# HGRN scores with the keys of two sequence tiles in one stationary operand, the odd tile's reversed

## The chip, the cores and the metric

The kernel runs on one core of one Trainium2 chip. The metric is device time in microseconds (us) of one execution, lower is better. Engines are named as in the profile: PE is TensorE (matrix products), PEld its weight loads, DVE is VectorE, ACT is ScalarE, POOL is GpSimd and SP is SyncE, which here only issues transfers. A product has a stationary operand, which is loaded into the array first, and a moving operand, which is streamed through it; the result goes to one of eight banks of PSUM, each 128 partitions by 512 float32 values.

## What is computed

The reference is a two-layer decoder trunk on x of shape 1 x 512 x 2048 (float32). Layer 0 runs two recurrent branches beside each other, RG-LRU and HGRN2; layer 1 is differential attention. The change is in the HGRN2 branch, with 16 heads of 128 key features and 128 value features:

```python
def hgrn2_chunkwise(q, k, v, log_f):
    ...
    def step(state, inp):
        qc, kc, vc, gc = inp
        b = jnp.cumsum(gc, axis=2)
        o_inter = jnp.einsum('bhtk,bhkv->bhtv', qc * jnp.exp(b), state)
        decay = jnp.exp(jnp.where(mask, b[:, :, :, None, :] - b[:, :, None, :, :], -jnp.inf))
        scores = jnp.einsum('bhtk,bhsk,bhtsk->bhts', qc, kc, decay)
        o = o_inter + jnp.einsum('bhts,bhsv->bhtv', scores, vc)
        b_last = b[:, :, -1:, :]
        state = (jnp.exp(b_last[:, :, 0, :, None]) * state
                 + jnp.einsum('bhsk,bhsv->bhkv', kc * jnp.exp(b_last - b), vc))
        return state, o
```

The score of query t and key s is a sum over the 128 features of q(t) k(s) exp(b(t) - b(s)), for s not after t. The decay depends on the feature, so that a plain product of queries and keys does not give it.

## The kernel before

**Tiling.** The 512 positions are four tiles of 128. Features lie on the partitions, positions on the columns, so that a work tile of a head is 128 x 512.

**The scores by levels.** `hgrn_head` (line 196) splits exp(b(t) - b(s)) at a position between s and t. At level h (32, 16, 8, 4, 2) the positions fall into pairs of neighbouring blocks of h; the first block of a pair holds keys, the second queries, and b at the last key splits the exponent. `decays(h)` (233) makes one tile `e` of 128 x 512 for a level: keys times their part of the decay in the key columns (DVE line 239), queries times theirs in the query columns (238 and 241), with one exponential for both (ACT, 240). `score_mm` (244) then multiplies, for levels 16 to 2, the 128 columns of each tile by themselves: stationary and moving operand are the same 128 columns, four products a level (254). Of the 128 x 128 results only key rows against query columns of the same pair are wanted; `score_out` (256) copies these into the head's score tile `st` under a mask `msk` (268). Level 32 has eight products of 32 keys by 32 queries (249) and two copies (260), and the step of 64 has four of 64 by 64 (337) and a copy by ACT (342). Neighbours (h = 1) and the diagonal come from products of a matrix of ones in the fp32r format (279 to 282), where the diagonal is taken out by the identity (284).

**What follows.** `kp` holds the keys for the state that goes on to the next tile; it is transposed (339) into `so`. The state is built from `so` and v (350), and the output from `st`, v, `qp` and the states (365, 367). The output is normed and transposed (383), and handed on as `yb`. In all of these float32 products the trace has two matmul records for one product in the code, and one for one transpose; a record is called a pass below.

**Where the work stands.** The weights come in chunks of 512 KB on SP's queue (`raw`, 80), and each half chunk is split by ACT and DVE into two fp32r parts (`split`, 87; lines 91 and 92). `proj_feat` (126) and `proj_tok` (141) run 12 products of 512 columns for one half chunk (lines 104 to 106) and then call `tick`, which lets the generators in `mids` take `ticks` steps; a `yield` ends a step. `hgrn` (393) runs over eight pairs of heads: three feature projections a pair, and for each even pair a token projection that makes v for four heads. The two heads of a pair are worked out during the projections of the next pair, 2.1 steps for a half chunk in odd pairs and 1.3 in even ones (line 407). A head has 24 steps. Instructions are emitted in this order, but the framework's planner sorts each engine's list anew from its own estimate of when each is ready, with the order of the program as priority (splits first); at run time each engine then keeps its list.

**The start.** x, transposed, is loaded into the buffers yb0 to yb7, from which the normed input is scaled into `h` (804, 805). `prepare` (157) loads x again, untransposed, through POOL's queue into the same buffers as they come free (167), squares it on ACT (168), and works out the norm; it waits 10 steps first, and 5 more before its transposes (182). The tables `cst` (798) and `msk` (810) go through SP's queue between the loads of x and the later weight chunks.

Of the kernel before, what the change touches and what calls it, by code (L numbers as in the profile page):

```python
# [19 lines left out]
P = 128  # L20
# [27 lines left out]
K_ID, K_COS, K_SIN, K_NEG = 0, 128, 192, 256  # L48
N_CST = 384


class Kernel:
# [104 lines left out]
    def prepare(self):  # L157
# [4 lines left out]
        for _ in range(10):  # L162
            yield
        for i in range(8):
            xt = self.ybp.tile([P, 2 * S], F32, name=f"yb{(i + 2) % 8}")
            t, hf = i // 2, i % 2
            nc.gpsimd.dma_start(xt, self.x[t * P:(t + 1) * P, hf * 1024:(hf + 1) * 1024])
            nc.scalar.activation(xt, xt, AF.Square, accum_out=ss0[:, i:i + 1])
            yield
# [8 lines left out]
        for _ in range(5):  # L178
            yield
# [16 lines left out]
    def hgrn_head(self, hd, qs, f, sg, v, vc):  # L196
# [6 lines left out]
        k = wk.tile([P, S], F32, name="k")  # L203
# [26 lines left out]
        def vw(t, h):  # L230
            return t.rearrange("p (n two h) -> p n two h", two=2, h=h)

        def decays(h):
            n = S // (2 * h)
            e = wk.tile([P, S], F32, name="e", bufs=3)
            e0, e1 = vw(e, h)[:, :, 0, :], vw(e, h)[:, :, 1, :]
            mid = vw(b, h)[:, :, 0, h - 1:h].broadcast_to([P, n, h])
            V.tensor_tensor(e1, vw(b, h)[:, :, 1, :], mid, op=ALU.subtract)
            V.tensor_tensor(e0, vw(lnk, h)[:, :, 0, :], mid, op=ALU.add)  # L239
# [4 lines left out]
        def score_mm(h, e, ps):  # L244
            if h == 32:
                for t in range(NT):
                    for o in (0, 64):
                        c = t * P + o
                        nc.tensor.matmul(ps[o:o + 32, t * 32:(t + 1) * 32], e[:, c:c + 32], e[:, c + 32:c + 64],
                                         start=True, stop=True)  # L250
                return
            for t in range(NT):
                sl = slice(t * P, (t + 1) * P)
                nc.tensor.matmul(ps[:, sl], e[:, sl], e[:, sl], start=True, stop=True)  # L254

        def score_out(li, h, ps):
            if h == 32:
                ev, pv = st.rearrange("p (a c) -> p a c", a=NT), ps.rearrange("p (a c) -> p a c", a=NT)
                for o in (0, 64):
                    V.tensor_copy(ev[o:o + 32, :, o + 32:o + 64], pv[o:o + 32])  # L260
                return
            n4 = P // (2 * h)

            def v4(t):
                return t.rearrange("p (a n two h) -> p a n two h", a=NT, two=2, h=h)[:, :, :, 1, :]

            mk = self.msk[:, li * 64:(li + 1) * 64].rearrange("p (n h) -> p n h", h=h)
            V.copy_predicated(v4(st), mk.unsqueeze(1).broadcast_to([P, NT, n4, h]), v4(ps))

        def bank():  # L270
# [5 lines left out]
        yield  # L276
        st = wk.tile([P, S], F32, name="st")
# [5 lines left out]
        score_mm(32, e32, p2[:, 256:384])  # L283
        V.tensor_tensor(st.rearrange("p (a c) -> p a c", a=NT), ps.rearrange("p (a c) -> p a c", a=NT),
                        self.ident.unsqueeze(1).broadcast_to([P, NT, P]), op=ALU.mult)
        V.copy_predicated(st.rearrange("p (a n two) -> p a n two", a=NT, two=2)[:, :, :, 1],
                          self.msk[:, 64 * len(LEVELS):].unsqueeze(1).broadcast_to([P, NT, 64]),
                          p2[:, 0:256].rearrange("p (a n) -> p a n", a=NT))
        score_out(0, 32, p2[:, 256:384])
# [3 lines left out]
        e4 = decays(4)  # L293

# [3 lines left out]
        kq = wk.tile([P, S], F32, name="e128")  # L298
        ke = kq[:, 0:256].rearrange("p (c t) -> p c t", t=64)
        qo = kq[:, 256:512].rearrange("p (c t) -> p c t", t=64)  # L300

        def c64(t):
            return t.rearrange("p (c two t) -> p c two t", two=2, t=64)

        yield
        ps, p2 = bank(), bank()
        score_mm(16, e16, ps)
        score_mm(8, e8, p2)
        score_out(1, 16, ps)
        score_out(2, 8, p2)  # L310
        yield
        e2 = decays(2)
        yield
        be = b.rearrange("p (c t) -> p c t", t=64)[:, :, 63]
        dc = sm.tile([P, 12], F32, name="dc")
        V.tensor_copy(dc[:, 0:8], be)
        V.tensor_tensor(dc[:, 8:12], be[:, 0:8:2], be[:, 1:8:2], op=ALU.add)
# [666 lines left out]
```

## Time and profile before

| | |
|---|---|
| median of 3 runs | 2590.29 us (2589.52 to 2590.51) |
| profiled execution | 2592.2 us, of which the profiled span is 2590.4 us |
| granted TensorE clock | 0.999 of full speed |
| ACT busy | 1254.9 us of the span |
| DVE busy | 1413.8 us of the span |

The durations below come from the profiled execution. A matmul's duration in the trace runs from its start to its modelled end; products overlap, so that the distance between two starts, not the duration, is what a product costs in a row of them.

### The profile page before, as it was taken

The page shows a single profiled execution, that of the slowest core. Times are in us where ns is not written, and L with a number is a line of the kernel's source. Part 1 is how long each engine was busy: PE and PEld are TensorE (multiplying, and loading weights), DVE is VectorE, ACT ScalarE, POOL GpSimd, SP SyncE. Part 2 cuts the span into 40 slices and gives each one's busy share as a digit, 9 for nine tenths or more (in the row PEclk, how much of TensorE's full clock was granted, in tenths as well). Part 3 has the DMA queues.
Part 4 walks back from the last instruction along what each step waited for, and adds up shares of the span by engine and source line. Part 5 has one row for each costly group of instructions (what it writes and reads, how often), then busy time and mean ns, then how long its engine had stood idle before and what let it go on. Part 6 is the DMA issues. An engine that isn't in the chain of part 4 may idle for free.

```text
span 2590.4 us, 33188 instructions
## 1 busy us (share of the span) xinstructions
PE 2572.1 (99%) x12416; PEld 2134.4 (82%) x12416; DVE 1413.8 (55%) x3074; ACT 1254.9 (48%) x2456; POOL 4.6 (0%) x12
## 2 busy tenths in 40 slices
PE   9999999999999999999999999999999999999999
PEld 6888888888888888888888888888888888888887
DVE  5475656556657666555554555344534534544654
ACT  7354545445445465455544444344434434434543
POOL 0000000000000000000000000000000000000000
PEclk9999999999999999999999999999999999999999
DMA  6222222222222232232233333222222222222243
GB/s 243 98 82 74 82 83 79 83 78 78 82 84 72 74 106 98 98 98 98 90 122 98 131 122 128 97 91 81 79 93 82 75 96 82 79 93 92 87 147 114
DMA packets 73889, 250.48 MB, mean 97 GB/s; under 512 B 8192, under 2 KB 8960, under 8 KB 73728
## 3 DMA queue, kind: packets, MB, share of 16 engines
q1 hardware_dynamic: 72000, 243.56, 28.0%
q0 software_dynamic: 1152, 4.19, 0.4%
q8 instruction: 97, 1.59, 0.3%
q10 hardware_dynamic: 576, 0.61, 0.1%
q14 instruction: 64, 0.52, 0.1%
HBM read 239.95 MB, written 8.39 MB: 96 GB/s over the span
## 4 chain that ended last, share of the span: by engine, by line
PE 95%; ACT 2%; DVE 1%; issue 1%; DMA 1%; SPq 0%; POOL 0%; DVEq 0%; ACTq 0%; POOLq 0%
PE pj L104 28%; PE pj L106 28%; PE pj L105 28%; PE pm L254 2%; PE pm L614 1%; PE pm L104 1%; PE pm L106 1%; PE pm L105 1%; PE pm L365 1%; ACT a L726 0%; PE pm L594 0%; PE pm L367 0%; PE pm L350 0%; PE pm L337 0%; PE pm L638 0%
## 5 line engine op out<-in xcount | busy, mean ns | idle before, releaser
L92 DVE TENSOR_TENSOR wlo<-wraw,whi 128x512 fp32r<-128x512 f32 x848 | 583.0, 689 | 727.6 <-ACT whi L91 709.1
L91 ACT CAST whi<-wraw 128x512 fp32r<-128x512 f32 x848 | 523.5, 618 | 813.0 <-PE pj L106 482.6
L104 PE MATMUL pj<-whi 128*128 128x512 f32 x768 | 299.6, 391 | 0.0
L106 PE MATMUL pj<-whi,wlo 128*128 128x512 f32 x768 | 299.6, 390 | 0.0
L105 PE MATMUL pj<-wlo,whi 128*128 128x512 f32 x768 | 299.2, 390 | 0.0
L104 PEld LDWEIGHTS pj<-whi 128*128 128x128 f32 x768 | 144.3, 188 | 30.2 <-issue 0.5
L106 PEld LDWEIGHTS pj<-whi,wlo 128*128 128x128 f32 x768 | 144.2, 188 | 30.2 <-DVE wlo L92 0.2
L105 PEld LDWEIGHTS pj<-wlo,whi 128*128 128x128 f32 x768 | 144.3, 188 | 29.3
L92 DVE TENSOR_TENSOR wlo<-ya,whi 128x512 fp32r<-128x512 f32 x64 | 44.3, 693 | 91.2 <-ACT whi L91 91.2
L240 ACT ACTIVATE e<-e 128x512 f32<-128x512 f32 x80 | 50.6, 632 | 88.6 <-DVE e L239 88.4
L91 ACT CAST whi<-ya 128x512 fp32r<-128x512 f32 x64 | 39.7, 621 | 100.9 <-PE pj L105 100.9
L92 DVE TENSOR_TENSOR wlo<-y,whi 128x512 fp32r<-128x512 f32 x64 | 44.2, 691 | 77.4 <-ACT whi L91 77.4
L91 ACT CAST whi<-y 128x512 fp32r<-128x512 f32 x64 | 39.9, 623 | 92.5 <-PE pj L105 90.1
L92 DVE TENSOR_TENSOR wlo<-yb,whi 128x512 fp32r<-128x512 f32 x64 | 44.2, 691 | 69.7 <-ACT whi L91 69.4
L91 ACT CAST whi<-yb 128x512 fp32r<-128x512 f32 x64 | 39.8, 621 | 78.3 <-PE pj L105 78.2
L254 PEld LDWEIGHTS pm<-e 128*128 128x128 f32 x512 | 62.1, 191 | 2.4
L254 PE MATMUL pm<-e 128*128 128x128 f32 x512 | 62.3, 275 | 0.0
L619 ACT ACTIVATE p<-pm,mx 128x128 f32<-128x128 f32 (+3 forms) x64 | 33.5, 527 | 34.3 <-DVE mx L617 29.5
L726 ACT ACTIVATE a<-pj,rstd 128x128 f32<-128x128 f32 x128 | 47.5, 421 | 0.5
L241 DVE TENSOR_TENSOR e<-e,hin 128x256 f32<-128x256 f32 x80 | 34.0, 425 | 22.1 <-ACT e L240 20.9
L616 DVE TENSOR_REDUCE mx<-pm 128x1 f32<-128x128 f32 (+3 forms) x64 | 29.6, 484 | 11.3 <-PE pm L615 11.3
L562 DVE SCALAR_TENSOR_TENSOR a<-a,rs_y,row 128x128 f32<-128x128 f32 x128 | 35.6, 347 | 0.0
(473 smaller groups left out, 6448.4 us busy)
## 6 DMA issues: line engine op xcount, KB each, us to landing
wraw<-in_w_rec SPq DMA_DIRECT2D x191, 512.0 KB, 3.3
wraw<-in_w_att SPq DMA_DIRECT2D x128, 512.0 KB, 3.2
wraw<-in_w_rout SPq DMA_DIRECT2D x64, 512.0 KB, 3.3
wraw<-in_w_aout SPq DMA_DIRECT2D x32, 512.0 KB, 3.3
yb<-in_x POOLq DMA_DIRECT2D x8, 512.0 KB, 7.4
wraw<-in_w_gate SPq DMA_DIRECT2D x8, 512.0 KB, 3.2
xo<-in_x SPq DMA_DIRECT2D x16, 256.0 KB, 4.6
x1d<-xo SPq DMA_DIRECT2D x16, 256.0 KB, 4.0
```

What stands on the lines that cost most here:

```text
L91: self.nc.scalar.copy(hi, src)
L92: self.nc.vector.tensor_tensor(lo, src, hi.bitcast(F32), op=ALU.subtract)
L104: mm(out, a[0], b[0], start=start, stop=False)
L105: mm(out, a[0], b[1], start=False, stop=False)
L106: mm(out, a[1], b[0], start=False, stop=stop)
L240: nc.scalar.activation(e, e, AF.Exp)
L241: V.tensor_tensor(e1, e1, vw(qs, h)[:, :, 1, :], op=ALU.mult)
L254: nc.tensor.matmul(ps[:, sl], e[:, sl], e[:, sl], start=True, stop=True)
L562: V.scalar_tensor_tensor(sl, sl, rs[:, t * 4 + g:t * 4 + g + 1], gain, op0=ALU.mult, op1=ALU.mult)
L616: V.tensor_reduce(mx[:, i:i + 1], ps[:, :n], axis=AX.X, op=ALU.max)
L619: nc.scalar.activation(e[:, :n], ps[:, :n], AF.Exp, scale=ATT_SCALE, bias=mx[:, i:i + 1], accum_out=z[:, i:i + 1])
L726: nc.scalar.activation(x[:, t, g * P:(g + 1) * P], ps[t][:, g * P:(g + 1) * P], AF.Square, scale=r1, accum_out=ss[:, t * 4 + g:t * 4 + g + 1])
```

## The change

Keys sit in every other block of h columns. Read backwards, the keys of a tile fall into the other blocks. So 64 keys of an even tile at their own places and 64 keys of the following odd tile, backwards, fill one stationary operand of 128 columns; the moving operand is the 64 queries of the one and the 64 of the other. One product then serves two tiles, at every level from 64 to 2, and a mask that is mirrored for the odd tile takes the wanted entries. The rows of the odd tiles in `st` and in `kp` are thereby backwards, so v's odd tiles are turned round too, once for four heads, by a product with a reversal matrix that is added to `cst`.

```diff
-K_ID, K_COS, K_SIN, K_NEG = 0, 128, 192, 256
-N_CST = 384
+K_ID, K_REV, K_COS, K_SIN, K_NEG = 0, 128, 256, 320, 384
+N_CST = 512
...
-        for _ in range(10):
+        for _ in range(14):
             yield
         for i in range(8):
-            xt = self.ybp.tile([P, 2 * S], F32, name=f"yb{(i + 2) % 8}")
+            xt = self.ybp.tile([P, 2 * S], F32, name=f"yb{(i + 5) % 8}")
...
-        for _ in range(5):
+        for _ in range(7):
             yield
...
-        k = wk.tile([P, S], F32, name="k")
+        k = wk.tile([P, S], F32, name="st")
...
+        def packed(e):
...
+            ev = e.rearrange("p (u x) -> p u x", u=2)
+            return ev[:, :, 0:P], ev[:, :, P:2 * P]
 
         def decays(h):
-            n = S // (2 * h)
             e = wk.tile([P, S], F32, name="e", bufs=3)
-            e0, e1 = vw(e, h)[:, :, 0, :], vw(e, h)[:, :, 1, :]
-            mid = vw(b, h)[:, :, 0, h - 1:h].broadcast_to([P, n, h])
-            V.tensor_tensor(e1, vw(b, h)[:, :, 1, :], mid, op=ALU.subtract)
-            V.tensor_tensor(e0, vw(lnk, h)[:, :, 0, :], mid, op=ALU.add)
+            ks, qu = packed(e)
+            n, m = P // (2 * h), P // h
+            qu = qu.rearrange("p u (m h) -> p u m h", h=h)
+            mid = vw(b, h)[:, :, :, 0, h - 1:h]
+            V.tensor_tensor(qu, vw(b, h)[:, :, :, 1, :], mid.broadcast_to([P, 2, m, h]), op=ALU.subtract)
+            for par, kv in ((0, ks), (1, ks[:, :, ::-1])):
+                mine = slice(par * n, (par + 1) * n)
+                V.tensor_tensor(kv.rearrange("p u (n two h) -> p u n two h", two=2, h=h)[:, :, :, 0, :],
+                                vw(lnk, h)[:, :, mine, 0, :], mid[:, :, mine, :].broadcast_to([P, 2, n, h]), op=ALU.add)
             nc.scalar.activation(e, e, AF.Exp)
-            V.tensor_tensor(e1, e1, vw(qs, h)[:, :, 1, :], op=ALU.mult)
+            V.tensor_tensor(qu, qu, vw(qs, h)[:, :, :, 1, :], op=ALU.mult)
             return e
...
-            for t in range(NT):
-                sl = slice(t * P, (t + 1) * P)
-                nc.tensor.matmul(ps[:, sl], e[:, sl], e[:, sl], start=True, stop=True)
+        def score_mm(e, ps):
+            ks, qu = packed(e)
+            for u in range(2):
+                nc.tensor.matmul(ps[:, u * P:(u + 1) * P], ks[:, u, :], qu[:, u, :], start=True, stop=True)
 
         def score_out(li, h, ps):
...
+            mk = self.msk[:, li * P:(li + 1) * P].rearrange("p (m h) -> p m h", h=h)
+            V.copy_predicated(vw(st, h)[:, :, :, 1, :], mk.unsqueeze(1).broadcast_to([P, 2, P // h, h]),
+                              ps.rearrange("p (u m h) -> p u m h", u=2, h=h))
...
-        score_mm(32, e32, p2[:, 256:384])
+        score_mm(e32, p2[:, 256:512])
...
+        score_out(len(LEVELS), 1, p2[:, 0:256])
+        score_out(0, 32, p2[:, 256:512])
...
-        V.tensor_tensor(kp.rearrange("p (c t) -> p c t", t=64), lnk.rearrange("p (c t) -> p c t", t=64),
-                        be.unsqueeze(2).broadcast_to([P, 8, 64]), op=ALU.add)
-        nc.scalar.activation(qp, b, AF.Exp)
+        for par, kv, kd in ((0, k64[:, :, 0:64], kt[:, :, 0, 1, :]), (1, k64[:, :, 127:63:-1], kt[:, :, 1, 0, ::-1])):
+            V.tensor_tensor(kv, l64[:, :, par, 0, :], be[:, :, par, 0, :].broadcast_to([P, 2, 64]), op=ALU.add)
+            V.tensor_tensor(kd, l64[:, :, par, 1, :], be[:, :, par, 1, :].broadcast_to([P, 2, 64]), op=ALU.add)
+        nc.scalar.activation(q64, b64[:, :, :, 1, :], AF.Exp)
         yield
-        nc.scalar.activation(ke, c64(kp)[:, :, 0, :], AF.Exp)
-        nc.scalar.activation(c64(kp)[:, :, 1, :], c64(kp)[:, :, 1, :], AF.Exp)
-        V.tensor_tensor(qo, c64(qp)[:, :, 1, :], c64(qs)[:, :, 1, :], op=ALU.mult)
+        nc.scalar.activation(k64, k64, AF.Exp)
+        mid64 = kp.rearrange("p (u x) -> p u x", u=2)[:, :, 64:192]
+        nc.scalar.activation(mid64, mid64, AF.Exp)
+        nc.scalar.activation(qt[:, :, :, 0, :], b64[:, :, :, 0, :], AF.Exp)
+        V.tensor_tensor(q64, q64, s64[:, :, :, 1, :], op=ALU.mult)
...
-        for t in range(NT):
-            nc.tensor.matmul(p3[0:64, t * 64:(t + 1) * 64], ke[:, t, :], qo[:, t, :], start=True, stop=True)
+        score_mm(e64, p2[:, 0:256])
...
+        for par in range(2):
+            rows = slice(par * 64, par * 64 + 64)
+            nc.scalar.copy(vw(st, 64)[rows, :, par, 1, :],
+                           p2[rows, 0:256].rearrange("p (u m t) -> p u m t", u=2, t=64)[:, :, par, :])
...
+    def reverse(self, v):
...
+        ps = [self.pm.tile([P, S], F32, name="pm") for _ in range(2)]
+        for i in range(2):
+            self.nc.tensor.matmul(ps[i], self.cst[:, K_REV:K_REV + P], v[:, 2 * i + 1, :], start=True, stop=True)
+        for i in range(2):
+            self.nc.scalar.copy(v[:, 2 * i + 1, :], ps[i])
+        yield
...
-            ticks = TICK_HG if pr == 0 else 2.1 if pr % 2 else 1.3
+            ticks = TICK_HG if pr == 0 else 2.3 if pr % 2 else 1.4
...
+                self.mids.append(self.reverse(v))
...
-                self.msk = self.wk.tile([P, 64 * (len(LEVELS) + 1)], I32, name="msk")
+                self.msk = self.wk.tile([P, P * (len(LEVELS) + 1)], I32, name="msk")
...
-        msk[:, li * 64:(li + 1) * 64] = (s // (2 * h) == t // (2 * h)) & (s % (2 * h) < h)
+        m = (s // (2 * h) == t // (2 * h)) & (s % (2 * h) < h)
+        msk[:, li * P:li * P + 64] = m
+        msk[:, li * P + 64:(li + 1) * P] = m[::-1]
```

`reverse` runs as the first step after a token projection, ahead of the two heads of that pair. `k` shares the buffer of `st`. A head still has 24 steps.

More of the change, by code (lines that the diff above doesn't have):

```diff
@@ L293, in hgrn_head @@
         e4 = decays(4)
-        kp = wk.tile([P, S], F32, name="kp")
-        qp = wk.tile([P, S], F32, name="qp")
[L298 to L303, printed above, removed]
-        yield
[L306 to L310, printed above, removed]
+        yield
+        ps = bank()
+        score_mm(e16, ps[:, 0:256])
+        score_mm(e8, ps[:, 256:512])
+        score_out(1, 16, ps[:, 0:256])
+        score_out(2, 8, ps[:, 256:512])
         yield
@@ L313, in hgrn_head @@
         yield
-        be = b.rearrange("p (c t) -> p c t", t=64)[:, :, 63]
+        kp = wk.tile([P, S], F32, name="kp")
+        qp = wk.tile([P, S], F32, name="qp")
+        e64 = wk.tile([P, S], F32, name="e128")
+        k64, q64 = packed(e64)
+        b64, l64, s64, kt, qt = (vw(t, 64) for t in (b, lnk, qs, kp, qp))
+        q64 = q64.rearrange("p u (m t) -> p u m t", m=2)
+        be = b64[:, :, :, :, 63:64]
         dc = sm.tile([P, 12], F32, name="dc")
-        V.tensor_copy(dc[:, 0:8], be)
@@ L334, in hgrn_head @@
[L334 to L337 removed]
+        ps, p2, p3 = bank(), bank(), bank()
+        score_mm(e4, ps[:, 0:256])
+        score_mm(e2, ps[:, 256:512])
+        score_mm(e64, p2[:, 0:256])
         for c in range(NT - 1):
[L339 removed]
+            nc.tensor.transpose(p3[:, c * P:(c + 1) * P], kp[:, c * P:(c + 1) * P], self.ident)
@@ L897, in constants @@
     cst[:, K_ID:K_ID + P] = np.eye(P, dtype=np.float32)
+    cst[:, K_REV:K_REV + P] = np.eye(P, dtype=np.float32)[::-1]
     pos = np.arange(S, dtype=np.float32)
@@ L904, in constants @@
     cst[:, K_NEG:K_NEG + P] = np.where(i[None, :] <= i[:, None], 0.0, -1e30)
-    msk = np.zeros((P, 64 * (len(LEVELS) + 1)), np.int32)
+    msk = np.zeros((P, P * (len(LEVELS) + 1)), np.int32)
     for li, h in enumerate(LEVELS + (1,)):
```

53 lines of the change are left out of this document (15 added, 38 removed).

## The prediction

> **What bounds the kernel now.** I read the page from the top: span, busy engines, granted clock, chain that ended last.
>
> ```profile
> span 2590.4 us, 33188 instructions
> PE 2572.1 (99%) x12416; PEld 2134.4 (82%) x12416; DVE 1413.8 (55%) x3074; ACT 1254.9 (48%) x2456; POOL 4.6 (0%) x12
> PEclk9999999999999999999999999999999999999999
> PE 95%; ACT 2%; DVE 1%; issue 1%; DMA 1%; SPq 0%; POOL 0%; DVEq 0%; ACTq 0%; POOLq 0%
> L91 ACT CAST whi<-wraw 128x512 fp32r<-128x512 f32 x848 | 523.5, 618 | 813.0 <-PE pj L106 482.6
> L92 DVE TENSOR_TENSOR wlo<-wraw,whi 128x512 fp32r<-128x512 f32 x848 | 583.0, 689 | 727.6 <-ACT whi L91 709.1
> ```
>
> PE is busy 99% of the time at the full clock and holds 95% of the chain; the splits of the weights (L91, L92) wait for PE, not PE for them. The change lies in the stage of the heads, 130 to 910 us, so I ask for the stage's windows, and for what PE waits for there.
>
> ```profile
> 130.00:910.00 780.00, 773.32 (x4174) 650.60 (x4173) 494.34 (x1159) 389.85 (x723) 0.00 (x0) 1.00 0.23 79
> PE pm L383 <- DVE kp L377: 5.7, 5, 1.4
> PE pm L350 <- ACT so L341: 1.0, 1, 1.0
> ```
>
> (Window, length, busy PE, PEld, DVE, ACT, POOL, clock, DMA share, GB/s.) PE waits 6.7 us of 780, while DVE works 494 and ACT 390. So PE time removed here is time removed, as long as the other engines keep up.
>
> **What a product costs.** Busy means are latencies; the price is the step between starts. From PE's timeline, in order: a block with 16 passes of level 4 and 2, 8 of the 64 step and 3 transposes (A); a block of 16 passes alone (B); the ones products with the 16 narrow passes of level 32 (C); passes of the output block (L365, L367).
>
> ```profile
> 303.11 1.95 PE L254 MATMUL pm<-e 128*128 128x128 f32 x16
> 304.99 0.68 PE L337 MATMUL pm<-e 128*64 128x64 f32 x8
> 305.60 0.55 PE L339 MATMUL pm<-cst,kp 128*128 128x128 f32 x3
> 305.90 0.48 PE L104 MATMUL pj<-whi,h6h 128*128 128x512 f32 x1
> 306.21 0.39 PE L105 MATMUL pj<-wlo,h6h 128*128 128x512 f32 x1
> ...
> 290.41 1.95 PE L254 MATMUL pm<-e 128*128 128x128 f32 x16
> 292.12 0.48 PE L104 MATMUL pj<-whi,h2h 128*128 128x512 f32 x1
> 292.43 0.39 PE L105 MATMUL pj<-wlo,h2h 128*128 128x512 f32 x1
> ...
> 344.42 0.39 PE L280 MATMUL pm<-e,ones 128*128 128x512 f32 x1
> 344.65 0.28 PE L281 MATMUL pm<-e,ones 128*128 128x256 f32 x1
> 344.77 0.28 PE L282 MATMUL pm<-e,ones 128*128 128x256 f32 x1
> 344.97 0.45 PE L249 MATMUL pm<-e 128*32 128x32 f32 x16
> 345.35 0.50 PE L104 MATMUL pj<-h6h,whi 128*128 128x512 f32 x1
> 345.69 0.40 PE L105 MATMUL pj<-h6l,whi 128*128 128x512 f32 x1
> ...
> 314.89 0.61 PE L365 MATMUL pm<-v,st 128*128 128x128 f32 x4
> 315.33 0.39 PE L367 MATMUL pm<-so,qp 128*128 128x128 f32 x2
> 315.55 0.39 PE L365 MATMUL pm<-v,st 128*128 128x128 f32 x2
> 315.78 0.39 PE L367 MATMUL pm<-so,qp 128*128 128x128 f32 x2
> ```
>
> Eight 128-wide float32 passes take 315.78 - 314.89 = 0.89, so p = 0.111 us each, with different operands on the two sides, as the change will have them. Block B, from its first start to the second projection product, takes 2.02 = 16 p + c, so c = 0.24 (of which 0.23 is the ordinary step).
>
> **The change on PE, per head.**
> - A: before 306.21 - 303.11 = 3.10. After: 2 products at each of levels 4, 2 and 64 are 12 passes, and 3 transposes: 15 p + c = 1.91. Saves **1.19**.
> - B: 4 products in place of 8, 8 p less. Saves **0.89**.
> - C: before, from L282 to the second projection product, 345.69 - 344.77 = 0.92. After: the step of a 256-column product (344.77 - 344.65 = 0.12), 4 passes, c: 0.80. Saves **0.12**.
>
> That is 2.20 a head, times 16 heads: **-35.2 us**.
>
> For C the Trainium skill has a rule that speaks against the change: the page "TensorEngine Tiling (Array Packing)", section "Performance Considerations", advises column tiling for narrow stationary operands (up to four times for 32). The narrow passes do cost little here (0.38 for 16); going by that alone, 4 p = 0.44 would lose 0.06 a head, 1 us in all. The row has what the rule leaves out, 0.20 ahead of the narrow block and 0.34 behind it, and I go by the row.
>
> **The reversal.** Four times (once for four heads) two float32 products of 512 columns, so 16 passes of a form that the trace lacks. Below: a 512-column fp32r product's step, 344.65 - 344.42 = 0.23, gives 16 x 0.23 = 3.7. Above: four 128-wide passes each, 0.444, gives 7.1. A float32 pass of 128 columns (0.111) costs what an fp32r product of 256 costs (0.12), so it seems to pay twice for a column; I take the upper end, **+7.1**.
>
> The Trainium skill has a rule for each end. "FP8 and Floating Point Precision", section "TensorE Precision Notes", counts four passes of the array for true float32, which agrees with twice a column in each of two records. "TensorE: Matmul & The Clock Gate", section "LDWEIGHTS (loading the stationary operand)", gives columns / 1.2 ns, 107 ns for 128: then 0.111 is the load, and a long product would hide it. No row before tells these apart.
>
> Does PE wait for the reversal's operand? It is placed behind the first half chunk after the token projection:
>
> ```profile
> 124.90 0.39 PE L104 MATMUL pj<-h0h,whi 128*128 128x512 f32 x1
> 125.63 0.68 ACT L428 ACTIVATE v<-pj,rcol 128x512 f32<-128x512 f32 x1
> ```
>
> That half chunk of 12 products ends its issue at 124.90 + 12 x 0.227 = 127.6; v's last tile is done at 126.3. No wait, with 1.3 to spare. The two copies back (0.69 each, as L428) have until the first use of v in line 350, many steps later.
>
> **The other engines.**
>
> ```profile
> L239 DVE TENSOR_TENSOR e<-lnk,b 128x256 f32<-128x256 f32 x77 | 32.9, 428 | 0.1
> L268 DVE COPY_PREDICATED st<-msk,pm 128x256 f32<-128x256 int32 x64 | 32.5, 508 | 2.6 <-ACT st L342 2.0
> L260 DVE COPY st<-pm 32x128 f32<-32x128 f32 x32 | 8.9, 277 | 0.2
> L221 DVE TENSOR_TENSOR so<-hin,k 128x512 f32<-128x512 f32 x15 | 10.4, 693 | 6.1 <-PE pm L367 6.1
> ```
>
> 512 elements cost 0.69 (L92), 256 cost 0.43, so 128 cost about 0.29 by the line through them. The key add becomes two of 128 at five levels: 5 x (0.58 - 0.43) = +0.75. At the 64 step four adds of 128 replace one of 512 (+0.47) and five products replace four (+0.16). One masked copy (0.51) replaces two copies of 0.28 (-0.05). DVE gets 1.3 us a head, ACT under 1 (one more copy into `st`, smaller exponentials, the copies back). A head has 780 / 16 = 48.8 us; DVE's share is 494 / 16 = 30.9 and grows to 32.2, while PE's falls to 46.6. Hidden by PE; without that cover it would be 21 us.
>
> `k` in `st`'s buffer adds a wait: the next head's exponential (ACT, 213) now follows the output products L365 of this head. Behind it on ACT stand the squares of L372 and the casts of L91. But DVE's L221, which needs `k`, already waits for L367 of the same block, so I cost it at nothing; bounds: 0 to 0.63 a head (one exponential ahead of the squares), 10 us if no step of slack takes it up. The steps per half chunk rise by about 8%, so a pair ends earlier and further from the next pair's first work, where the 5.7 us of waits at L383 lie. They may go, or double with the changed order: -5.7 to +5.7, I take 0.
>
> **The start.**
>
> ```profile
> 22.73 1.06 ACT L168 ACTIVATE yb<-yb 128x1024 f32<-128x1024 f32 x1 [3.48 <-DMA yb<-in_x]
> 24.55 0.50 PE L104 MATMUL pj<-h10h,whi 128*128 128x512 f32 x1 [2.45 <-ACT h10h L804]
> 30.20 0.53 PE L104 MATMUL pj<-h12h,whi 128*128 128x512 f32 x1 [2.06 <-ACT whi L91]
> 11.41 0.53 POOL L167 DMA_DIRECT2D yb<-in_x  x1 [3.33 <-DVE h3l L805]
> 15.25 0.53 POOL L167 DMA_DIRECT2D yb<-in_x  x1 [3.31 <-DVE h5l L805]
> GB/s 243 98 82 74 82 83 79 83 78 78 82 84 72 74 106 98 98 98 98 90 122 98 131 122 128 97 91 81 79 93 82 75 96 82 79 93 92 87 147 114
> ```
>
> ACT stands 3.48 us before a square of the second x load, with the casts of h10 behind it, and PE stands 2.45 and then 2.06. Loads go out as buffers come free: yb0, yb1 (11.41, after h3), yb2 (15.25, after h5). With i + 2 the first load in the program is yb2, the third to go out; with i + 5 the program's order agrees with the buffers', and the square taken first can be one that has landed. Against that, `cst` and `msk` grow by 0.26 MB ahead of a weight chunk: at 243 GB/s 1.1 us. Bounds -4.5 to +1.1; I take the first stall gone less the longer tables, 1.1 - 2.45 = **-1.4**.
>
> **Sum.** -35.2 + 7.1 - 1.4 = -29.5. The profiled execution takes 2592.2 (span 2590.4 and 1.8 around it): 2562.7. The median shown, 2590.3, lies 1.9 below it: **2560.8 us**. With the bounds of the start, of the waits at L383 and of `k`'s wait, which will hardly all fall to one side, the forecast's own range is 2552 to 2571.
>
> **Rivals.**
> - *The reversal is cheap* (0.23 a pass): 3.4 less, **2557.4**. For it: the load rule; against: twice a column fits both widths.
> - *New waits at the scores.* PE stands before each of the three blocks of a head because DVE's chain (add, exponential, product) grew by an instruction that is issued in line. If each loses 0.3 us (the length of the new add): 48 x 0.3 = 14.4, **2575**. Against: 6.7 us of waits in the stage now, and steps of slack between a level and its product.
> - *The time is not on PE's path*: the projections are fed too slowly to go faster, **2590**. Against: L91 waits on PE and DMA is at 0.23 of its time.
> - *Slower:* adds that write backwards (7 a head) cost DVE far more than 0.29. DVE sets the pace above 46.6 us a head and the kernel is slower than before above 48.8, which needs (48.8 - 32.2) / 7 = 2.4 us more for each. At 3 us each in all: 30.9 + 1.3 + 7 x 2.7 = 51.1 a head, 37 us more than before, **2627**. Nothing in the trace writes backwards; against it, the strided adds of L239 (level 2 to 32 in one group) have one mean.
>
> **Chances.** Forecast 0.68, cheap reversal 0.13, new waits 0.11, not on the path 0.04, slower 0.04. The range 2553 to 2574 holds the first two and part of the third. About 0.2% (5 us) is what a measurement of this kernel can tell from no change: faster 0.91, same 0.05, slower 0.04.
>
> **What would show it.** 512 records of matmuls fewer in the scores and 16 more in the reversal (12416 to 11920); blocks A, B and C at 1.9, 1.1 and 0.8; steps of 0.44 between the reversal's passes; PE's waits from 130 to 910 us still under 12; DVE's busy time in the heads' stage up by about 21. It is wrong if PE's idle time grows by more than 10 us or a 128-wide pass no longer takes 0.111.

## The result, and the profile after

The changed kernel takes 2559.53 us (median of 4 runs, 2558.81 to 2559.65) where the kernel before took 2590.34 (4 runs beside them, 2589.52 to 2590.51): a ratio of 0.9881, 95% interval 0.9864 to 0.9898. 2560.8 us was forecast. The profiled span falls by 32.6 us, from 2590.4 to 2557.8.

The head of the page of the kernel after, and the window of the heads' stage with what PE waits for, there and (last two rows, us in total, times, longest) in the whole run:

```profile
span 2557.8 us, 32354 instructions
PE 2542.4 (99%) x11920; PEld 2106.9 (82%) x11920; DVE 1406.9 (55%) x3202; ACT 1262.3 (49%) x2496; POOL 4.6 (0%) x12
...
130.00:910.00 780.00, 779.25 (x3828) 651.93 (x3828) 512.12 (x1321) 415.00 (x792) 0.00 (x0) 1.00 0.27 84
PE pm L382 <- DVE kp L376: 0.2, 1, 0.2
...
PE pj L104 <- ACT whi L91: 6.6, 1, 6.6
PE pj L104 <- ACT h2h L813: 1.3, 1, 1.3
```

PE is still the bound, at the full clock, with the 11920 records forecast. In the stage of the heads it now has 0.75 us free in 780, less than the 6.7 before. L376 and L382 are the norm's scaling and transposes, 377 and 383 before. At the start there is one long wait of 6.6 us for a split (L91), where there were 2.45 and 2.06; the wait for `h2h`, 0.3 before, is 1.3 here.

PE's timeline after, at the places that answer to A, B, C and the reversal (L258 are the score products, 254 before; L336 the transposes of `kp`; L278 the last ones product; L396 the reversal):

```profile
292.32 1.50 PE L258 MATMUL pm<-e 128*128 128x128 f32 x12
293.65 0.49 PE L336 MATMUL pm<-cst,kp 128*128 128x128 f32 x3
...
294.21 0.40 PE L105 MATMUL pj<-wlo,h4h 128*128 128x512 f32 x1
...
280.51 1.05 PE L258 MATMUL pm<-e 128*128 128x128 f32 x8
...
281.63 0.39 PE L105 MATMUL pj<-wlo,h0h 128*128 128x512 f32 x1
...
339.96 0.28 PE L278 MATMUL pm<-e,ones 128*128 128x256 f32 x1
340.07 0.61 PE L258 MATMUL pm<-e 128*128 128x128 f32 x4
...
340.75 0.40 PE L105 MATMUL pj<-h6l,whi 128*128 128x512 f32 x1
...
332.18 1.88 PE L396 MATMUL pm<-v,cst 128*128 128x512 f32 x4
...
334.13 0.40 PE L105 MATMUL pj<-h2l,whi 128*128 128x512 f32 x1
```

From the first start of each block to the second projection product: A 294.21 - 292.32 = 1.89, B 1.12, C 0.79, where 1.91, 1.13 (2.02 - 0.89) and 0.80 were forecast. The same reading over all 16 heads has means of 1.206, 0.893 and 0.126 us saved, 2.225 a head, **-35.6 us**. The reversal takes 334.13 - 332.18 = 1.95 less an ordinary step of 0.23, so 1.72 for four passes, 0.43 each, **+6.9 us** for four times.

The other two places where the time moved are the waits at the norm's transposes and the start. Before, then after, PE's first product of the second projection:

```profile
37.39 0.39 PE L104 MATMUL pj<-h0h,whi 128*128 128x512 f32 x1
```

```profile
38.70 0.39 PE L104 MATMUL pj<-h0h,whi 128*128 128x512 f32 x1
```

| term | forecast, us | measured in the profiles, us |
|---|---|---|
| score products | -35.2 | -35.6 |
| reversal | +7.1 | +6.9 |
| start, to the second projection | -1.4 | +1.3 |
| waits in the heads' stage | 0 | -6.5 (6.7 to 0.2) |
| sum | -29.5 | -33.9, of a span that fell by 32.6 |

1.3 us are left over and not assigned. 0.5 of them lie between the start of the third projection and the end of the first token projection, which takes 65.7 us after and 65.3 before; the other 0.8 lie behind it. In the profiles the sum is 3.1 us off, because two small terms were missed with opposite signs, by +2.7 and -6.5; the medians differ by 1.3 only since the profiled execution of before lay 1.9 above its median. These two terms are what the experiments are about, together with three costs that the prediction could only bound or take from rows nearby: the reversal, DVE's new work and the narrow products.

### The profile page after: what moved, and what is told of

It reads as the page before. It is cut to its first block, busy times and chain, and to the rows that moved or that the text cites. A ratio compares the mean times of both kernels' runs of the same rounds, so it can differ in the third digit from the quotient of the medians.

```text
span 2557.8 us, 32354 instructions
## 1 busy us (share of the span) xinstructions
PE 2542.4 (99%) x11920; PEld 2106.9 (82%) x11920; DVE 1406.9 (55%) x3202; ACT 1262.3 (49%) x2496; POOL 4.6 (0%) x12
## 4 chain that ended last, share of the span: by engine, by line
PE 96%; ACT 2%; DMA 1%; DVE 1%; issue 0%; SPq 0%; DVEq 0%; ACTq 0%
PE pj L104 29%; PE pj L106 29%; PE pj L105 29%; PE pm L258 2%; PE pm L623 1%; PE pm L104 1%; PE pm L106 1%; PE pm L105 1%; DMA wraw<-in_w_rec 1%; ACT a L735 1%; PE pm L364 1%; PE pm L603 0%; PE pm L366 0%; PE pm L349 0%; PE pm L382 0%; PE pm L647 0%
## 5 line engine op out<-in xcount | busy, mean ns | idle before, releaser
L91 ACT CAST whi<-wraw 128x512 fp32r<-128x512 f32 x848 | 523.3, 618 | 788.3 <-PE pj L106 490.4
L91 ACT CAST whi<-ya 128x512 fp32r<-128x512 f32 x64 | 39.7, 621 | 100.9 <-PE pj L105 100.9
L91 ACT CAST whi<-y 128x512 fp32r<-128x512 f32 x64 | 39.9, 623 | 92.5 <-PE pj L105 90.0
L91 ACT CAST whi<-yb 128x512 fp32r<-128x512 f32 x64 | 39.8, 621 | 78.3 <-PE pj L105 78.2
L262 DVE COPY_PREDICATED st<-msk,pm 128x256 f32<-128x256 int32 x96 | 51.3, 535 | 2.0 <-ACT st L341 0.8
L258 PEld LDWEIGHTS pm<-e 128*128 128x128 f32 x384 | 49.1, 191 | 2.5
L258 PE MATMUL pm<-e 128*128 128x128 f32 x384 | 50.5, 274 | 0.0
L249 DVE TENSOR_TENSOR e<-lnk,b 128x128 f32<-128x128 f32 x160 | 44.1, 286 | 0.0
L104 PE MATMUL pj<-h12h,whi 128*128 128x512 f32 x80 | 32.9, 411 | 6.6 <-ACT whi L91 6.6
```

The source lines that it names most:

```text
L91: self.nc.scalar.copy(hi, src)
L104: mm(out, a[0], b[0], start=start, stop=False)
L249: V.tensor_tensor(kv.rearrange("p u (n two h) -> p u n two h", two=2, h=h)[:, :, :, 0, :], vw(lnk, h)[:, :, mine, 0, :], mid[:, :, mine, : ...
L258: nc.tensor.matmul(ps[:, u * P:(u + 1) * P], ks[:, u, :], qu[:, u, :], start=True, stop=True)
L262: V.copy_predicated(vw(st, h)[:, :, :, 1, :], mk.unsqueeze(1).broadcast_to([P, 2, P // h, h]), ps.rearrange("p (u m h) -> p u m h", u=2, h=h))
```

## The experiments

Each time below is a median beside runs of the kernel before on the same chip, the ratio is to those. "After" is the changed kernel. The kernel before had medians from 2590.14 to 2591.17 beside the different runs, so that differences of less than 1 us between kernels of different runs say nothing. Line numbers of edited kernels can stand one or two later.

### The start: is it the larger tables, or when x is loaded again?

The trace of after shows what happened at the start. ACT's and PE's timeline, then POOL's:

```profile
19.44 1.06 ACT L168 ACTIVATE yb<-yb 128x1024 f32<-128x1024 f32 x1 [0.18 <-DMA yb<-in_x]
30.85 1.14 ACT L91 CAST whi<-wraw 128x512 fp32r<-128x512 f32 x2 [3.10 <-DMA wraw<-in_w_rec]
31.52 0.80 PE L104 MATMUL pj<-h12h,whi 128*128 128x512 f32 x1 [6.56 <-ACT whi L91]
22.95 0.53 POOL L167 DMA_DIRECT2D yb<-in_x  x1 [3.26 <-DVE h11l L814]
```

The first stall did go as forecast: ACT waits 0.18 us for x at the second square where it had waited 3.48. But PE then runs into the fourth weight chunk, which has not landed: ACT waits 3.10 us for it. Because h10 and h11 came earlier, the load of x that waits for h11 went out at 22.95, and the one behind it followed. In the trace of before it stands here:

```profile
26.23 0.53 POOL L167 DMA_DIRECT2D yb<-in_x  x1 [6.72 <-DVE h11l L805]
```

And the transfer view from 8 to 40 us has the weights' median from issue to landing, before and after:

```profile
wraw<-in_w_rec SPq DMA_DIRECT2D x6, 512.0 KB, 7.8
```

```profile
wraw<-in_w_rec SPq DMA_DIRECT2D x6, 512.0 KB, 10.1
```

So the theory is that x, wanted late, and the weights, wanted now, share the transfer engines, and the new order of x puts more of it ahead of the chunk. The rival is the 0.26 MB of larger tables that stand ahead of it. The first kernel keeps the tables and takes back the steps and the order of the loads:

```diff
-        for _ in range(14):
+        for _ in range(10):
...
-            xt = self.ybp.tile([P, 2 * S], F32, name=f"yb{(i + 5) % 8}")
+            xt = self.ybp.tile([P, 2 * S], F32, name=f"yb{(i + 2) % 8}")
...
-        for _ in range(7):
+        for _ in range(5):
```

> The changed kernel with the start of before: 10 steps ahead of the x loads, buffers in the order i + 2, 5 steps ahead of the transposes. Theory (collision): in the changed kernel the stall ahead of h10 is gone, but the x loads then go out 3 us earlier and fall on the fourth weight chunk, which is what PE waits for at h12. So here the stall ahead of h10 comes back (about 2.5 us), the x loads on POOL at yb5 and yb6 go out late again (26 and 27.5 us), the wait at h12 shrinks to 2 to 3 us, and the second projection starts near 38 us (37.4 before, 38.7 with the change): the time is 0 to 1 us below the changed kernel's 2559.5. Rival (the new order is worth its stall, as predicted): 1.4 to 2.5 us above it.

Measured: 2557.12 us (2556.36 to 2558.21), ratio 0.9871 (0.9855 to 0.9888). PE's waits and the first product of the second projection there:

```profile
PE pj L104 <- ACT h10h L813: 3.1, 1, 3.1
...
35.88 0.39 PE L104 MATMUL pj<-h0h,whi 128*128 128x512 f32 x1
```

The stall ahead of h10 is back at 3.1 us, the wait at h12 is gone although the tables are still the large ones, and the second projection starts 2.8 us earlier than after. The median is 2.4 us lower, more than the 0 to 1 expected, and the ranges of the two kernels' runs do not touch. The tables are not the cause, and the new start is a small loss in place of a gain. Its size is less sure than its sign. With the old start the second projection begins at 37.39 (before), 35.88 (this kernel) and 35.62 (a kernel below that does not touch the start); with the new one, in six profiles of this document without x held, from 36.95 to 39.07. The 37.39 of before is the late one of its three, so +1.3 is rather too small for the loss.

If x is in the way, holding it back must give more than either order. The next kernel holds the second loads until the last tile of `h` is written, by a write to each buffer that reads that tile:

```diff
+            V.tensor_copy(xt[:, 0:1], self.hT[KD - 1][1][:, 0:1].bitcast(F32))
             nc.gpsimd.dma_start(xt, ...)
```

> The changed kernel with every second load of x held until the last tile of h is made (one column is written from it ahead of the load). Theory (collision): the fourth weight chunk, issued at 14 us, no longer shares the transfer engines with some 2.6 MB of x and lands by 25 us in place of 30.8; PE goes from h11 to h12 without the 6.6 us wait, and the second projection starts near 32 us in place of 38.7: 2552 to 2554 us. Rival (the chunk is late of itself or by the larger tables): the wait stays above 4 us and the time within 2 us of 2559.5. Second rival (the norm comes too late for the third projection): PE waits near 55 us and gives back part.

Measured: 2554.16 us (2553.78 to 2555.13), ratio 0.9859 (0.9845 to 0.9874). POOL's and PE's timeline:

```profile
25.85 4.30 POOL L168 DMA_DIRECT2D yb<-in_x  x8 [25.41 <-DVE neg_b L191]
26.08 0.50 PE L104 MATMUL pj<-h12h,whi 128*128 128x512 f32 x1 [1.60 <-ACT whi L91]
31.66 0.39 PE L104 MATMUL pj<-h0h,whi 128*128 128x512 f32 x1
54.98 0.50 PE L104 MATMUL pj<-h0h,whi 128*128 128x512 f32 x1 [0.91 <-DVE hin L412]
```

All eight loads go out at 25.85, the product of h12 starts 5.4 us earlier than after, the second projection 7.0 earlier. The cast of the fourth chunk starts at 25.41 without a wait for its load, where it starts at 30.85 after. 1.6 us of the 7.0 don't reach the end; of these the wait at 54.98 shows 0.9, where the third projection is now late because the norm's x lands late. That the early loads of x hold up the weight chunk is thereby shown.

### The waits at the norm's transposes: steps, or `k` in `st`'s buffer?

The prediction left it to the steps per half chunk whether the 5.7 us at L383 go or double. The first kernel is after with the steps of before:

```diff
-            ticks = TICK_HG if pr == 0 else 2.3 if pr % 2 else 1.4
+            ticks = TICK_HG if pr == 0 else 2.1 if pr % 2 else 1.3
```

> The changed kernel with 2.1 and 1.3 steps for a half chunk as before. Theory (the steps took the waits away): the waits of PE for DVE ahead of the transposes of a pair's last head (6.7 us before, 0.2 with the change) come back, 4 to 7 us, 2564 to 2566 us. Rival (the shorter score blocks or DVE's new order took them away): no such waits, within 1 us of 2559.5.

Measured: 2559.46 us (2558.75 to 2560.79), ratio 0.988 (0.9865 to 0.9895), and the wait at L382 stays at 0.2 us. The steps do nothing to this wait. The counterpart is before with the new start and the new steps (14 and 7 steps, i + 5; 2.3 and 1.4):

> The kernel before with only the schedule of the change: 14 steps, buffers i + 5, 7 steps, and 2.3 and 1.4 steps for a half chunk; scores, tables and v as before. Theory: PE's waits in the heads' stage fall from 6.7 to under 1.5 us; at the start the stall ahead of h10 goes and the wait at h12 grows, together -1 to +1 us: 2583 to 2586 us. Rival (the waits went with the scores, not with the steps): 2589 to 2592.

Measured: 2592.01 us (10 runs, 2590.63 to 2592.88), ratio 1.0006 (0.9996 to 1.0015), no difference that can be told, and not the 2583 to 2586 of the theory. Its waits, whole run:

```profile
PE pm L383 <- DVE kp L377: 5.7, 5, 1.4
PE pj L104 <- ACT whi L91: 5.3, 1, 5.3
```

The wait at L383 stands unchanged (only the 1.0 us at L350 is gone), and the long wait at the start has come along with the new start, on a kernel with the small tables. What remains for L383 is the score change itself or the shared buffer. The third kernel is before with that edit alone:

```diff
-        k = wk.tile([P, S], F32, name="k")
+        k = wk.tile([P, S], F32, name="st")
```

> The kernel before with one edit: k in the buffer of st. Theory (buffer): the next head's early work on ACT and DVE can no longer run ahead of this head's output products, so it no longer stands in DVE's list ahead of the norm of a pair's last head; PE's waits ahead of the transposes fall from 5.7 to under 1 us: 2584 to 2586 us. Rival (DVE's list came out another way by the new work in decays): the waits stay, 2589 to 2591 us.

Measured: 2585.61 us (10 runs, 2585.01 to 2587.26), ratio 0.9981 (0.9971 to 0.999). What PE waits for from 130 to 910 us:

```profile
PE pm L383 <- ACT whi L91: 0.5, 1, 0.5
PE pm L383 <- DVE kp L377: 0.2, 1, 0.2
```

6.7 us have become 0.7: the edit that was costed at nothing, with a bound of 10 us on the side of loss, is a gain of about 5. (The median is 5.6 us lower than that of before beside it. In the profiles, the time from the end of the first token projection to the end of the span falls from 2465.5 to 2460.4, by 5.1, although the waits fall by 6.0; the 0.9 between them is not explained, and a like 0.8 stood among the 1.3 left over above.) Why can be read in DVE's list around one of the four places where PE waited 1.4. Before (the last row is PE's):

```profile
205.85 0.69 DVE L209 SCALAR_TENSOR_TENSOR lf<-hin,lf 128x512 f32<-128x512 f32 x1 [1.08 <-ACT lf L208]
206.46 0.15 DVE L122 SCALAR_TENSOR_TENSOR rs_y<-rs_t,rs_y 128x4 f32<-128x4 f32 x1
206.65 0.69 DVE L377 TENSOR_TENSOR kp<-pm,rs_y 128x512 f32<-128x512 f32 x1
207.49 0.63 PE L383 MATMUL pm<-cst,kp 128*128 128x128 f32 x4 [1.36 <-DVE kp L377]
```

And with `k` in `st`'s buffer:

```profile
205.50 0.68 DVE L377 TENSOR_TENSOR kp<-pm,rs_y 128x512 f32<-128x512 f32 x1
...
209.78 0.68 DVE L209 SCALAR_TENSOR_TENSOR lf<-hin,lf 128x512 f32<-128x512 f32 x1
```

L209 is the first DVE instruction of a head that is still to come. It waits 1.08 us for ACT's logarithm (L208), and in the list of before it stands ahead of the end of this head's norm (L122, L377), for which PE waits 1.36. A wait in a list holds up what is behind it, whether that needs it or not. With the shared buffer the planner puts L209 behind the norm here and at the other three such places, and PE's wait is gone. (At three more places L209 stands as close ahead of a norm in both kernels, and there PE does not wait.) In the trace of after no L209 stands less than 16 us ahead of a norm; at the same place:

```profile
203.14 0.68 DVE L376 TENSOR_TENSOR kp<-pm,rs_y 128x512 f32<-128x512 f32 x1
...
206.19 0.68 DVE L209 SCALAR_TENSOR_TENSOR lf<-hin,lf 128x512 f32<-128x512 f32 x1
```

The wait that the prediction looked for is there too, and costs nothing that shows: in after ACT stands 10.4 us in all for L364, the output products, ahead of L213. Why the planner's estimate tips this way was not followed. After was not run with a buffer of its own for `k`, so for after the cause is shown by the list and by the edit on before, not by an edit on after.

The same kernel gives a check of the large terms, since it has the waits gone and the old scores. From the first product behind the first token projection (123.15 us there, 126.68 after) to the end of the span it takes 2460.4 us, after 2431.1: 29.2 less. The blocks and the reversal make 35.6 - 6.9 = 28.7, and its waits in the heads' stage are 0.5 longer (0.7 against 0.2). (It is also the kernel whose start moved without an edit there: this product stood at 124.90 before.)

### The reversal: its price, and a cheaper one

The forecast chose 0.444 for a float32 pass of 512 columns against 0.23; 0.43 was measured. To see whether the format sets it, v's odd tiles are split into two fp32r parts as they come out of the projection, and the two are multiplied by an fp32r reversal matrix into one bank:

```diff
-            self.nc.tensor.matmul(ps[i], self.cst[:, K_REV:K_REV + P], v[:, 2 * i + 1, :], start=True, stop=True)
+            self.nc.tensor.matmul(ps[i], self.rev, parts[i][0], start=True, stop=False)
+            self.nc.tensor.matmul(ps[i], self.rev, parts[i][1], start=False, stop=True)
...
+                    nc.scalar.activation(hi, ps[t], AF.Identity, scale=rc)
+                    nc.vector.scalar_tensor_tensor(lo, ps[t], rc, hi.bitcast(F32), op0=ALU.mult, op1=ALU.subtract)
```

> The changed kernel with the reversal in fp32r: v's odd tiles are split into two fp32r parts as they leave PSUM (ACT and DVE), and the reversal matrix, in fp32r too, is multiplied with both parts. Theory (a float32 pass pays twice for a column: 0.43 us for 512): four products of 0.23 us replace four passes of 0.43; a reversal falls from 1.72 to about 0.92 us, four of them 3.2 us: 2556 to 2557 us. Rival (the split, 0.7 us more of DVE for each odd tile, makes PE wait at the reversal or at the freed banks): within 1 us of 2559.5 or above.

Measured: 2555.16 us (2554.3 to 2556.41), ratio 0.9861 (0.9846 to 0.9876). PE's timeline:

```profile
329.13 0.39 PE L396 MATMUL pm<-kp,rev 128*128 128x512 f32 x1
329.36 0.39 PE L397 MATMUL pm<-qp,rev 128*128 128x512 f32 x1
...
330.05 0.39 PE L104 MATMUL pj<-h2h,whi 128*128 128x512 f32 x1
```

Four records again, but at steps of 0.23: 330.05 - 329.13 = 0.92 in place of 1.72, 3.2 us for four times. The medians differ by 4.4 us. From the first product behind the first token projection to the end the span is 3.1 us shorter than after's (2428.0 against 2431.1), which is the reversal; the rest lies ahead of it, where the second projection came 1.75 earlier in this profile (36.95), and is not shown to be a merit of the reversal.

The Trainium skill's page "FP8 and Floating Point Precision", section "TensorE Precision Notes", with four passes of the array for true float32, is what the trace bears out: a float32 record costs 1.9 times the fp32r record of as many columns. The Trainium skill's page "TensorE: Matmul & The Clock Gate", section "LDWEIGHTS (loading the stationary operand)", gives columns / 1.2 ns for a load, 107 ns for 128. The rival that the prediction drew from it, a long pass at 0.23, is refuted by the 0.43. Whether the load also stands behind the 0.111 of a 128-wide pass is open: twice a column gives as much there (0.43 / 4 = 0.108). A version that reverses v by its stationary operand, without a product of its own, was not tried.

### DVE: how much cover is there?

In the groups of the page of after, the key adds (half of them written backwards) and the masked copies:

```profile
L262 DVE COPY_PREDICATED st<-msk,pm 128x256 f32<-128x256 int32 x96 | 51.3, 535 | 2.0 <-ACT st L341 0.8
L249 DVE TENSOR_TENSOR e<-lnk,b 128x128 f32<-128x128 f32 x160 | 44.1, 286 | 0.0
```

The add takes 0.286 us on the mean of forward and backward ones, where 0.29 was estimated (the line through the two rows gives 0.30); all 160 lie between 0.269 and 0.335. To ask what DVE's cover is worth, the key adds of the five levels are each done twice:

```diff
-                V.tensor_tensor(kv.rearrange(...)...)
+                for _ in range(2):
+                    V.tensor_tensor(kv.rearrange(...)...)
```

> The changed kernel with every key add of the five levels done twice, ten more DVE instructions of 0.29 us for a head, 46 us of DVE in all. Theory (hidden by PE): PE's waits in the heads' stage stay under 2 us, the time within 1.5 us of 2559.5. Rival (PE stands at the scores when DVE's chain grows): 16 heads with three blocks each lose 0.3 to 0.9 us a block, 14 us or more: 2574 us or above.

Measured: 2567.32 us (2566.68 to 2567.72), ratio 0.9907 (0.9893 to 0.9922), 7.8 us slower than after. PE's waits in the whole run, and DVE's list at the norm of the same head as above, near 205 us:

```profile
PE pm L383 <- DVE kp L377: 7.0, 6, 1.5
PE pj L104 <- DVE hin L412: 1.4, 1, 1.4
...
204.45 0.69 DVE L92 TENSOR_TENSOR wlo<-wraw,whi 128x512 fp32r<-128x512 f32 x1 [1.18 <-ACT whi L91]
205.06 0.68 DVE L377 TENSOR_TENSOR kp<-pm,rs_y 128x512 f32<-128x512 f32 x1
```

Neither theory has it. No wait appears at the score blocks, where the rival looked for it. The 160 extra adds of 0.286 are 46 us of DVE's time and cost 7.8, of which 6.8 lie at the norm's transposes again: this time a split that waits for ACT stands in the list close ahead of L377, at five of the six places. So in this kernel the cover is not a matter of DVE's share alone but of what stands ahead of the one instruction that PE waits for.

### The narrow products of level 32

By the rule of the Trainium skill's page "TensorEngine Tiling (Array Packing)", section "Performance Considerations", narrow stationary operands want column tiling (products side by side in separate column quarters of the array). Before had them in two column quarters. Here level 32 of after goes back to 16 passes of 32 columns, spread over all four:

```diff
-        score_mm(e32, p2[:, 256:512])
+        for u in range(2):
+            for m, o in enumerate((0, 64, 96, 32)):
+                nc.tensor.matmul(p2[o:o + 32, 256 + u * 32:288 + u * 32], ks[:, u, o:o + 32],
+                                 qu[:, u, m * 32:(m + 1) * 32], start=True, stop=True)
...
-        score_out(0, 32, p2[:, 256:512])
+        for m, o in enumerate((0, 64, 96, 32)):
+            V.tensor_copy(vw(st, 32)[o:o + 32, :, m, 1, :], ...)
```

> The changed kernel with level 32 in narrow products again: eight of 32 keys by 32 queries for a head, now in all four column quarters of the array, and four copies of 32 rows in place of one masked copy. Theory (the edges of a narrow block cost more than its passes): the block with the ones products rises from 1.14 us to 1.2 to 1.27 us, 16 heads 1 to 2 us: 2560.5 to 2561.5 us. Rival (the rule of the Trainium skill, that narrow stationary operands are best packed beside each other): the block falls under 1.1 us and the time by 1 us or more.

Measured: 2559.87 us (2559.63 to 2560.15), ratio 0.9879 (0.9864 to 0.9894). PE's timeline:

```profile
340.30 0.28 PE L278 MATMUL pm<-e,ones 128*128 128x256 f32 x1
340.50 0.33 PE L282 MATMUL pm<-e 128*32 128x32 f32 x16
340.77 0.50 PE L104 MATMUL pj<-h6h,whi 128*128 128x512 f32 x1
341.10 0.40 PE L105 MATMUL pj<-h6l,whi 128*128 128x512 f32 x1
```

The 16 passes take 340.77 - 340.50 = 0.27, and 0.38 in two quarters before: the packing is real. But 0.20 ahead of them and 0.33 behind them stay as they were, where the ordinary steps are 0.12 and 0.23: 0.18 more at the edges. The block takes 341.10 - 340.30 = 0.80, and 0.79 with four wide passes (0.44 for the passes). The two forms cost the same; what the packing saves, 0.17, the edges take back. Neither the loss of the theory nor the gain of the rival came.

### Together

After with x held, the fp32r reversal and 5 steps (not 7) ahead of the norm's transposes:

> The changed kernel with three edits together: the second loads of x held until the last tile of h is made, the reversal in fp32r, and 5 steps in place of 7 ahead of the transposes of the norm, so that the third projection no longer waits for it. If the gains add up: 2554.2 (x held) less 3.2 (reversal) less about 1.3 (the wait at the third projection): 2549 to 2551 us. Rival (they share one slack): 2552 us or above.

Measured: 2549.80 us (2549.2 to 2550.71), ratio 0.9842 (0.9827 to 0.9858). It is the fastest of all, 9.7 us under after. The two parts alone make 5.4 + 4.4 = 9.8, but that they add up is partly chance, since the 4.4 held a shift of the start that cannot come again once x is held. In the profiles it reaches the first product behind the first token projection at 120.80, with x held alone at 120.88: the wait at the third projection is gone, but one at the norm's transposes stands in its place.

```profile
PE pm L183 <- DVE xr L178: 1.2, 1, 1.2
```

From there to the end it is 3.3 us shorter than with x held alone (2428.1 against 2431.4), which is the reversal. The same with the whole old start (10 steps, i + 2, 5 steps):

> As the kernel before this one, with the whole start of before (10 steps, buffers i + 2, 5 steps) under the held loads. Theory: once the loads are held, the numbers of the start only shift priorities: within 1 us of it, 2549 to 2552 us. Rival (the numbers still decide the order of the squares): 2 us or more apart.

Measured: 2557.46 us (2557.05 to 2558.24), ratio 0.9872 (0.9856 to 0.9888). Its gain is gone in one wait:

```profile
49.75 1.12 PE L183 MATMUL pm<-cst,xr 128*128 128x128 f32 x4 [6.20 <-DVE xr L178]
```

The transposes of x's norm stand too early in PE's list for loads that come late, and everything on PE stands behind them. At last the two edits of the schedule on the kernel before, x held and `k` in `st`'s buffer, with its 10 and 5 steps:

> The kernel before with the two edits that have nothing to do with the scores: k in the buffer of st, and the second loads of x held. Theory (the score change is worth its blocks of PE, 28.7 us, and the rest of the measured 30.8 came from the schedule): 2585.6 less 5 to 6: 2579 to 2581 us, which lies 24 to 27 us above the changed kernel with x held (2554.2) if the wait at the third projection is in that one alone, and 28 to 29 us above it if not. Rival (the gains of the schedule need the new scores): 2584 us or above.

Measured: 2587.84 us (10 runs, 2586.71 to 2588.58), ratio 0.9989 (0.9979 to 0.9999). The 2579 to 2581 of the theory did not come; it is no better than the buffer alone (2585.61), for the reason just seen:

```profile
PE pm L183 <- DVE xr L178: 4.5, 1, 4.5
```

In these kernels, holding a load pays in full only if what needs it is moved back with it.

## Why the prediction was right, point by point

- **PE is the bound**: right. It holds 99% of the span on both sides, and PE time taken away was time taken away: 28.7 us of blocks and reversal and 0.5 of waits, 29.2 us of span, in the comparison with the kernel that differs in little else.
- **A, B and C at 0.111 us a pass**: right, to 0.4 us in 35. That different stationary and moving operands cost as one operand used twice was read from the output block and holds.
- **C's choice of the row against the column rule**: right, 0.126 for 0.12. Four quarters of the array make the narrow passes cheaper than the two of before, and the edges still take it back.
- **The reversal at the upper end**: right, 6.9 for 7.1, by the reason given (twice a column in each record). No wait at its operand appeared. The rival of a cheap reversal is refuted; its price of 0.23 is that of an fp32r pass.
- **The start at -1.4**: wrong. The step that failed is "the first stall gone less the longer tables". The stall went, and the tables cost nothing that shows, but the step took no account of what earlier tiles of `h` set free: x loads that go out while the fourth weight chunk is on its way. Measured +1.3; with the old start on after, PE is 2.8 earlier and the median 2.4 lower. Up to 1.8 of such a shift is seen between kernels whose start is the same, so the sign is the firmer part.
- **The waits at L383 at 0**: wrong in size, -5.5, at the edge of the bounds of 5.7, and the 1.0 at L350 went too. The step that failed is the one that named the steps per half chunk: they do nothing to this wait (two runs). What does is the place of L209 in DVE's list.
- **`k` in `st`'s buffer at nothing**: wrong in sign. The wait that it adds was looked for as a loss, bounds 0 to 10 us; what it did to the order of DVE's list was not considered, and that was a gain of about 5 us in the kernel before (ratio 0.9981), the one that went into the row above.
- **DVE and ACT hidden by PE**: right, with the work itself put too high. The window shows DVE 17.8 us up and ACT 25, but it now holds more of the program (1321 instructions of DVE for 1159, where the whole run has only 128 more). By the lines of the heads in the whole run DVE rises from 339.8 to 352.0 us, 12 where 21 were forecast, and ACT, without its table loads, from 181.7 to 191.4, 10 where up to 16 were allowed. The rivals of new waits at the scores and of backward adds did not come; the doubled adds show that the next cost of DVE's work would have come at the norm instead.

That the total came out 1.3 us under the forecast is no evidence for the start and the waits: two misses of opposite sign, and a profiled execution of before that lay above its median, nearly cancelled. That part is luck.

## What to carry to other kernels

On a PE-bound kernel, price each block from start to start, its edges to the next full-width product included; here the sum of 48 blocks held to 0.4 us in 35. Narrow products have to be charged for their edges. Where lists are sorted by a planner and kept at run time, sharing or splitting a buffer moves instructions, and its effect has to be looked for in what then stands ahead of the instruction that PE waits for. When a stall near the start is taken away, ask which transfers that lets out earlier and whose they delay; hold back data that is wanted later, and move its consumer back with it.

## What was not expected of the hardware

- A float32 record of 512 columns costs 0.43 us and an fp32r record of 512 columns 0.23, so that splitting one operand in two and using fp32r nearly halves the reversal's time on PE with the same count of records (1.72 to 0.92). The other operand, the reversal matrix, holds only zeros and ones and needs no split; where both are split, as in the projections, this kernel runs three products.
- Narrow passes of 32 columns get cheaper with more column quarters in use, 0.38 us for 16 in two and 0.27 in four, but the 0.20 ahead and 0.33 behind (0.12 and 0.23 are ordinary) do not shrink.
- DVE's adds that write backwards cost about as much as those that write forwards: 0.286 us for 128 columns on the mean of both, and none of the 160, half of them backwards, above 0.335.
